# The second FFN of a transformer layer: eight blocks of ten, not five, by seven products for eight

## The chip, the cores and the metric

The kernel runs on one core of a Trainium2 chip. The metric is the device time of one execution in microseconds (us). TensorE (PE) multiplies matrices, VectorE (DVE) and ScalarE (ACT) work on tiles element by element, GpSimd (POOL) and SyncE (SP) here mostly issue transfers (DMA). SBUF is the memory on the chip, PSUM the small memory in banks into which TensorE sums.

## The reference

One layer of a diffusion backbone, width 2048, with 256 context tokens and 256 latent tokens: a half step of a gated FFN, a token mixer (attention heads and mLSTM heads), another half step FFN, and an RMSNorm. Each part is modulated by shift, scale and gate vectors (`mod`, nine of them) made from a condition vector. The change is about the second FFN, which is computed for the 256 latent tokens alone:

```python
def adaln(x, g, mod, i):
    return rms_norm(x, g) * (1 + mod[:, i + 1, None, :]) + mod[:, i, None, :]

def half_step_ffn(x, mod, i, g, w_up, w_down):
    h = adaln(x, g, mod, i)
    a, b = jnp.split(h @ w_up, 2, axis=-1)
    return x + 0.5 * mod[:, i + 2, None, :] * ((jax.nn.silu(a) * b) @ w_down)
```

`w_up` is 2048 x 11264 and `w_down` 5632 x 2048, in fp32. `mod` vector 8 is the gate of the second FFN.

## The kernel before

**Numbers.** An fp32 operand is kept as the sum of two parts: `hi`, a rounded copy, and `lo`, the rest. A product of two operands takes three matmuls (`mm3`, L145 to L149: hi by hi, hi by lo, lo by hi). Weights arrive by DMA in pieces of 128x2048 (1024 KB, tile `raw`, three buffers); `split` (L117) makes from each half a `hi` by ScalarE (L125) and a `lo` by VectorE (L126). There are four buffers of each, so two whole pieces. `load_split` (L138) does the load and the split, and steps one item of whatever stands in `beside["load"]`.

**Order.** The program is written out by hand with generators: a main loop goes through units of TensorE's work, and side generators are stepped at each of them (`steps`, `drain`, `weave`). A scheduler then puts each engine's instructions in an order that is fixed before the run.

**Modulation vectors.** A `mod` vector is a product of the condition with its own weights; it is computed by VectorE in 32 items of 128x1024 (`mod_half`, L200; the operation is on L205, with a read of its accumulator). Vectors 5 to 7 are computed beside the mixer by the class `Beside` (L271): 96 items, each with a DMA of 512 KB into one of a few slots (`fetch`, L287), paced by the table `PACE` of (item, step) pairs over 188 steps. The items and their loads are pinned in the order of the program. Vector 8 is computed in the second FFN, by `mod_late` (L264): 32 items in `beside["load"]`.

**The mixer** (about 1346 to 1945 us) projects, runs convolutions, the mLSTM and the attention, and ends in an output projection. Small operations of it that the change touches: the scaling of the mLSTM's values (`vw`, L1429), the copy of its state (L1434), the scaling of its queries (`mqT`, L1552), the scaling of attention's probabilities (L1699), and a copy of the heads' output (`cx`, L1750), all by VectorE.

**The second FFN** (L1935 to L2310) has 5632 hidden channels in eleven blocks of 512. Block 0 starts while the mixer ends; block 10 is finished last, with the final norm. Each block needs an up projection (two matrices a and b, 2048 x 512 each) and a down projection (512 x 2048, four pieces).
- `up(n)`: eight units, each one weight piece and 24 matmuls of 128x512; the two halves of the 256 tokens go to two banks. 192 matmuls.
- `quad(n)`: the same by seven products for eight, after Strassen and Winograd, on quarters of the tokens and channels: the weights come as sums of quarters. The seven products are a11, a12, n1, s4, s2, s3, a22, in this order, each in two steps of 12 matmuls (one weight piece of 128x2048 for each), so 14 steps and 168 matmuls. They sum in two banks X and Y (`psx`, one buffer each): a11 in X; a12 in Y; n1 in Y, s4 added in Y; s2 and s3 added in X; a22 in Y. After each product the bank is read: X copied by ScalarE (p1), Y added to it by VectorE (c11), Y copied by ScalarE (`cy`, L2098, kept), copied again (p35), X added by VectorE (c12), X added by VectorE and copied by ScalarE (c22), Y added by VectorE (c21), with silu and products in between (L2084, L2085, L2094, L2117).
- The weight sums of a quad are made by DMA: two tiles `chain` are loaded by SP, and GpSimd issues loads that add to them (`accum`, L735): three sums for the chain and one for the tile `ra`, for each of two pieces, so eight a quad. The first load of the next quad's chain is issued at the end (`again`).
- `turned` (L2051 on) transposes a block's result by TensorE and splits it into `hid2h` (ScalarE, L2066) and `hid2l` (VectorE, L2068, L2070); these tiles have two buffers.
- `down(n)`: four units of 24 matmuls; each pair of banks is added to `acc2` by VectorE (L2208), eight adds of 128x512 a block (block 0 is copied by ScalarE).

PSUM has four banks `mm`, two `tr` for the transposes, X and Y. The quads are the odd blocks 1 to 9, the `up` blocks 2, 4, 6, 8, 10. The main loop goes through 73 units of up and down, and `PACE2 = 70 / 73` puts one of the 70 quad steps behind each unit.

Of the kernel before, what the change touches and what calls it, by code (L numbers as in the profile page):

```python
# [19 lines left out]
P = 128  # L20
D = 2048
# [14 lines left out]
PACE = (4, 2), (12, 13), (19, 19), (26, 28), (33, 37), (37, 44), (42, 51), (48, 54), (52, 61), (55, 70), (58, 76), (59, 85), (63, 96)  # L36
PACE += (70, 102), (72, 109), (75, 118), (76, 130), (77, 144), (80, 152), (83, 163), (85, 166), (86, 174), (96, 181)

PACE2 = 70 / 73
# [17 lines left out]
def tile_layer(ctx: ExitStack, tc: tile.TileContext, I: dict, out: bass.AP):  # L57
# [205 lines left out]

    def mod_late(sp, i0, i1, pace):  # L264

        cB = sp.tile([P, 1024], F32, name="cBl", bufs=1)
        cond = Conditions(lambda h: h, lambda h: conditions({LAT: cB}, h, h + 1, (LAT,)), lambda h: {LAT: cB})
        raws = lambda: sp.tile([P, 1024], F32, tag="sraw", name="sraw", bufs=2)
        return mod_items(half_items(i0, i1), nc.sync.dma_start, raws, 2, cond, None, pace)
# [989 lines left out]
    with ExitStack() as mx:  # L1259
# [31 lines left out]
        N_EARLY, N_MIXER = 50, 85  # L1291

        early2 = one([P, 2, 1024], "early2", tag="mqT")
        tiles = [(mm.tile([P, 1024], F32, name="sr0"), 96)] + [(mm2.tile([P, 1024], F32, name=f"sr{j}"), N_MIXER) for j in (1, 2)]
        tiles += [(x, N_EARLY) for x in (early2[:, 0, :], early2[:, 1, :], one([P, 1024], "early1", tag="rt"))]
        mods = Beside(mm, 5, 8, tiles, PACE)
# [122 lines left out]
        def state(h, kTc):  # L1419
# [7 lines left out]
            for t in range(2):  # L1427
                for d in range(2):
                    nc.vector.tensor_scalar(vw[:, t, d, :], v1[CTX][t][:, h, :], wg[:, t, d, h : h + 1], None, op0=ALU.mult)  # L1429
# [4 lines left out]
            nc.vector.tensor_copy(C1[:, h, :, :], b[:, :260].rearrange("p (d c) -> p d c", d=2))  # L1434
# [39 lines left out]
        def latents():  # L1474
            held = {}
            for h in range(NH + 1):
                if h < NH:
# [31 lines left out]
                    nc.vector.tensor_tensor(A, A, mqT[:, h, :].unsqueeze(1).to_broadcast([P, 2, T]), op=ALU.mult)  # L1509
                    for d in range(2):  # L1510

                        for w, p0 in ((slice(0, 2), 0), (slice(2, 3), 3)) if d == 0 else ((slice(0, 1), 0), (slice(1, 3), 2)):
                            e_ = E[:, d, w, :]
                            nc.vector.tensor_tensor(e_, e_, pS.rearrange("p (q c) -> p q c", q=4)[:, p0 : p0 + w.stop - w.start, :], op=ALU.mult)
# [26 lines left out]
        for h in range(NH):  # L1541
# [8 lines left out]
            nc.scalar.activation(y, y, AF.Silu)  # L1550

            nc.vector.tensor_scalar(mqT[:, h, :], y, ISQ, None, op0=ALU.mult)  # L1552
# [130 lines left out]
        def attention(kv):  # L1683
            items = [(t, g) for t in range(2) for g in range(4)]
            pr, pT, o = {}, {}, {}
            for i in range(len(items) + 2):
                if i < len(items):
# [11 lines left out]
                    nc.vector.tensor_scalar(p, p, sd, None, op0=ALU.mult)  # L1699
# [42 lines left out]
        def mlstm_cat(c):  # L1742

            for t in range(2):
# [5 lines left out]
                nc.vector.tensor_copy(cxs[c, t], tb)  # L1750
# [36 lines left out]
        mods.more([(late2[:, 0, :], 96), (late2[:, 1, :], 96), (one([P, 1024], "late1", tag="C1"), 96)], nc.sync)  # L1787
# [147 lines left out]
    with f2x:  # L1935
        def hid_tiles():

            return [f2.tile([P, FB, T], F32R, tag=g, name=g) for g in ("hid2h", "hid2l")]
# [47 lines left out]
        acc2 = f2.tile([P, 2, D], F32, name="acc2", bufs=1)  # L1986
        chain_ = [f3.tile([P, 2048], F32, tag=f"c{q}", name=f"chain2{q}") for q in range(2)]
        f8cm = pool(name="f8", bufs=1)
        beside["load"] = mod_late(f8cm.__enter__(), 8, 9, ((32, 62),))
# [3 lines left out]
        QUADS = range(1, LAST, 2)  # L1993
# [57 lines left out]
        def turned():  # L2051
# [4 lines left out]
            if n >= 2 and n - 2 not in summed or n - 1 not in hids or (n - 1, 0) in [x[:2] for x in turn] or (n - 1, 1) in [x[:2] for x in turn]:  # L2056
                return
            turn.pop(0)
            if n not in hids:
                hids[n] = hid_tiles()  # L2060
# [18 lines left out]
        def ca_tile():  # L2079
            return f2b.tile([P, CB], F32, tag="ca", name="ca")  # L2080

        def quad(n):
# [26 lines left out]
            def c22():  # L2109
                assert (n, 0) in done  # L2110
# [13 lines left out]
            def again(q):  # L2124
                if n + 2 in QUADS:
                    nc.sync.dma_start(chain_[q], part(n + 2, 0, q))

            def loaded(q):
                ra[q] = ra_tile()
# [278 lines left out]
```

## Time and profile before

| what | us |
| --- | --- |
| median of 3 runs (least to most) | 2613.49 (2612.78 to 2615.28) |
| the profiled execution, its span from first to last instruction | 2612.7 |
| TensorE busy in it | 2590.1 |
| VectorE busy | 2119.7 |
| ScalarE busy | 1364.8 |
| mixer, output projection and start of the second FFN | about 1346 to 1945 |
| main part of the second FFN and final norm | about 1945 to 2613 |

The profiled execution has no time of its own beside its span. Its granted clock is 0.996 of full speed. The profile has a page (busy time by engine, the chain of work that ended last, groups of instructions by line) and a trace that can be asked for waits, stretches of time and timelines. In a row of a group stand the line, the engine, the operation with output and inputs and their sizes, the count, then the busy time in us and the mean of one in ns, then the engine's idle time ahead of them and what ended it. In a row of a line stand the least, median and longest duration in ns. In a row of waits stand the total in us, the number and the longest. Matmuls overlap in the pipeline, so their distance from start to start counts, not their length.

### The profile page before, as it was taken

The numbers are of one execution on the slowest core, as the hardware profiler recorded it, in microseconds if no ns is written. First come the engines' busy times: TensorE is split into PE (matmuls) and PEld (weight loads), VectorE is DVE, ScalarE is ACT, GpSimd is POOL, SyncE is SP. The second block draws the span as 40 slices with busy tenths as digits, with TensorE's granted clock in tenths as the row PEclk, the third lists the DMA queues.
The fourth block names the chain that finished last, engine by engine and source line by source line (L and its number), as shares of the span: only waits on it lengthen the run. The fifth ranks groups of instructions, "written<-read, shape, count | busy, mean of one in ns | idle before, by whom it ended". The sixth has DMA issues, their size and how long they took to land.

```text
span 2612.7 us, 33775 instructions
## 1 busy us (share of the span) xinstructions
PE 2590.1 (99%) x12742; PEld 2158.4 (83%) x12742; DVE 2119.7 (81%) x2860; ACT 1364.8 (52%) x1734; POOL 205.2 (8%) x261
## 2 busy tenths in 40 slices
PE   8999999999999999999999999999999999999998
PEld 5788888888888888888889889888898888888887
DVE  7788888878888788888887879788888777777867
ACT  4454444454444465444454337555576655555554
POOL 0000000100000100010110000120000000000001
PEclk8999999999999999999999999999999999999999
DMA  9989999999999998889987856665679998989975
GB/s 389 353 215 266 280 273 274 257 273 284 265 277 277 271 246 237 231 200 232 231 247 262 300 193 236 220 214 208 236 254 302 309 293 278 286 285 283 270 231 174
DMA packets 127219, 679.97 MB, mean 260 GB/s; under 512 B 14152, under 2 KB 16712, under 8 KB 65232
## 3 DMA queue, kind: packets, MB, share of 16 engines
q1 hardware_dynamic: 99696, 500.59, 51.6%
q0 software_dynamic: 27360, 177.22, 34.7%
q8 instruction: 100, 1.64, 0.2%
q14 instruction: 63, 0.52, 0.1%
HBM read 659.87 MB, written 17.89 MB: 259 GB/s over the span
## 4 chain that ended last, share of the span: by engine, by line
PE 92%; DVE 3%; DMA 2%; issue 1%; ACT 1%; POOL 0%; ACTq 0%; POOLq 0%; SPq 0%; DVEq 0%
PE mm L147 24%; PE mm L149 24%; PE mm L148 24%; PE mm L85 2%; PE tr L147 2%; PE tr L149 2%; PE tr L148 2%; PE Y L149 1%; PE Y L147 1%; PE Y L148 1%; PE tr L85 1%; PE X L147 1%; PE X L149 1%; PE X L148 1%; DVE lo L126 1%
## 5 line engine op out<-in xcount | busy, mean ns | idle before, releaser
L125 ACT ACTIVATE hi<-raw 128x1024 fp32r<-128x1024 f32 (+3 forms) x536 | 556.4, 1042 | 594.7 <-PE mm L149 435.4
L126 DVE TENSOR_TENSOR lo<-raw,hi 128x1024 fp32r<-128x1024 f32 (+1 forms) x524 | 632.1, 1211 | 272.3 <-ACT hi L125 246.9
L125 ACT ACTIVATE hi<-chain 128x1024 fp32r<-128x1024 f32 x320 | 338.0, 1059 | 257.3 <-PE mm L149 133.9
L126 DVE TENSOR_TENSOR lo<-chain,hi 128x1024 fp32r<-128x1024 f32 x320 | 386.5, 1221 | 85.4 <-ACT hi L125 82.3
L147 PE MATMUL mm<-hi,hhi 128*128 128x512 f32 (+3 forms) x1024 | 393.8, 385 | 0.0
L148 PE MATMUL mm<-lo,hhi 128*128 128x512 f32 (+3 forms) x1024 | 386.8, 378 | 0.0
L149 PE MATMUL mm<-hi,hlo 128*128 128x512 f32 (+3 forms) x1024 | 386.8, 378 | 0.0
L205 DVE SCALAR_TENSOR_TENSOR junk<-sraw,cBh 128x1024 fp8e5<-128x1024 f32 x192 | 234.4, 1221 | 16.8 <-DMA sraw<-in_w_mt 14.4
L149 PEld LDWEIGHTS mm<-hi,hlo 128*128 128x128 f32 x1024 | 192.5, 188 | 33.9
L147 PEld LDWEIGHTS mm<-hi,hhi 128*128 128x128 f32 x1024 | 192.6, 188 | 31.0
L148 PEld LDWEIGHTS mm<-lo,hhi 128*128 128x128 f32 x1024 | 192.8, 188 | 30.6
L149 PE MATMUL mm<-hi,hid2l 128*128 128x512 f32 x352 | 137.4, 390 | 0.0
L147 PE MATMUL mm<-hi,hid2h 128*128 128x512 f32 x352 | 137.2, 390 | 0.0
L148 PE MATMUL mm<-lo,hid2h 128*128 128x512 f32 x352 | 137.1, 389 | 0.0
L148 PE MATMUL mm<-lo,h2hi 128*128 128x512 f32 x320 | 124.9, 390 | 0.6 <-DVE lo L126 0.6
L147 PE MATMUL mm<-hi,h2hi 128*128 128x512 f32 x320 | 124.8, 390 | 0.0
L149 PE MATMUL mm<-hi,h2lo 128*128 128x512 f32 x320 | 124.6, 389 | 0.0
L735 POOL DMA_DIRECT2D chain<-in_w_up1b x60 | 53.1, 886 | 726.4 <-DVE lo L126 699.5
L147 PE MATMUL mm<-hhi,hi 128*128 128x512 f32 (+1 forms) x288 | 101.1, 351 | 0.0
L149 PE MATMUL mm<-hhi,lo 128*128 128x512 f32 (+1 forms) x288 | 99.0, 344 | 0.0
L148 PE MATMUL mm<-hlo,hi 128*128 128x512 f32 (+1 forms) x288 | 98.8, 343 | 0.0
L205 DVE SCALAR_TENSOR_TENSOR sr<-sr,cBl 128x1024 f32<-128x1024 f32 x65 | 78.4, 1219 | 9.0 <-DMA sr<-in_w_mt 9.0
(517 smaller groups left out, 5466.9 us busy)
## 6 DMA issues: line engine op xcount, KB each, us to landing
raw<-in_w_dn SPq DMA_DIRECT2D x70, 1024.0 KB, 7.7
sraw<-in_w_mt SPq DMA_DIRECT2D x128, 512.0 KB, 7.7
chain<-in_w_up1b POOLq DMA_DIRECT2D x60, 1024.0 KB, 10.4
raw<-in_w_up2b SPq DMA_DIRECT2D x50, 1024.0 KB, 6.9
raw<-in_w_up1b SPq DMA_DIRECT2D x40, 1024.0 KB, 7.7
mraw<-in_w_m SPq DMA_DIRECT2D x32, 1024.0 KB, 7.8
sr<-in_w_mt SPq DMA_DIRECT2D x62, 512.0 KB, 5.4
chain<-in_w_dn POOLq DMA_DIRECT2D x30, 1024.0 KB, 9.4
```

What stands on the lines that cost most here:

```text
L85: ins = getattr(self.engine, name)(*a, **k)
L125: scalar[0].activation(hi, src, AF.Copy)
L126: vector[0].tensor_tensor(lo, src, hi.bitcast(F32), op=ALU.subtract)
L147: tensor[0].matmul(out_ap, sh, mh, start=first, stop=False, skip_group_check=skip)
L148: tensor[0].matmul(out_ap, sh, ml, start=False, stop=False, skip_group_check=skip)
L149: tensor[0].matmul(out_ap, sl, mh, start=False, stop=last, skip_group_check=skip)
L205: ins = nc.vector.scalar_tensor_tensor(junk() if junk else raw, raw, 1.0, cB[s], op0=ALU.mult, op1=ALU.mult, accum_out=mT[:, i, s, kt, h : ...
L735: accum = lambda dst, src: nc.gpsimd.dma_start(dst, src, accum_op=ALU.add)
```

## The change

- The quads are blocks 1, 2, 4, 5, 6, 7, 8, 9; `up` is left for blocks 3 and 10. The main loop has 48 units: up(3), down of 0 and 1, of 2 and 3, of 4 and 5, up(10), down of 6 and 7. After two units, 112 quad steps are spread over the other 46. The last down, of 8 and 9, follows.
- `down` takes two blocks and sums both in one pair of banks, so that `acc2` is added to half as often.
- One of a quad's weight sums is made by VectorE (`ahead` loads `ra` early, `summed_half` adds it to the chain in halves of 128x1024, at the steps listed in `between`). A quad has six adding DMAs for eight.
- `hid2h` and `hid2l` have three buffers, `ca` three.
- Vector 8 is computed in the mixer: `Beside` has 128 items for 96, with a new `PACE`; `mod_late` goes.
- In the mixer `vw`, the state copy, the probabilities' scale and `cx` go to ScalarE; the queries' scale is put into two operations of VectorE that follow anyway.

```diff
+N_HID = 3
...
+PACE = (4, 2), (12, 13), (19, 19), (27, 28), (35, 37), (41, 44), (49, 51), (56, 54), (62, 61), (67, 70), (70, 76), (71, 85), (76, 96)
+PACE += (83, 102), (87, 109), (91, 118), (94, 130), (97, 144), (101, 152), (107, 163), (110, 170), (128, 181)
...
-PACE2 = 70 / 73
...
-        N_EARLY, N_MIXER = 50, 85
+        N_EARLY, N_MIXER = 62, 109
...
-        mods = Beside(mm, 5, 8, tiles, PACE)
+        mods = Beside(mm, 5, 9, tiles, PACE)
...
-                    nc.vector.tensor_scalar(vw[:, t, d, :], v1[CTX][t][:, h, :], wg[:, t, d, h : h + 1], None, op0=ALU.mult)
+                    nc.scalar.activation(vw[:, t, d, :], v1[CTX][t][:, h, :], AF.Copy, scale=wg[:, t, d, h : h + 1])
...
-            nc.vector.tensor_copy(C1[:, h, :, :], b[:, :260].rearrange("p (d c) -> p d c", d=2))
+            nc.scalar.activation(C1[:, h, :, :], b[:, :260].rearrange("p (d c) -> p d c", d=2), AF.Copy)
...
-                    nc.vector.tensor_tensor(A, A, mqT[:, h, :].unsqueeze(1).to_broadcast([P, 2, T]), op=ALU.mult)
+                    nc.vector.scalar_tensor_tensor(A, A, ISQ, mqT[:, h, :].unsqueeze(1).to_broadcast([P, 2, T]), op0=ALU.mult, op1=ALU.mult)
...
-            nc.vector.tensor_scalar(mqT[:, h, :], y, ISQ, None, op0=ALU.mult)
+            nc.scalar.activation(mqT[:, h, :], y, AF.Silu)
...
-                    nc.vector.tensor_scalar(p, p, sd, None, op0=ALU.mult)
+                    nc.scalar.activation(p, p, AF.Copy, scale=sd)
...
-                nc.vector.tensor_copy(cxs[c, t], tb)
+                nc.scalar.activation(cxs[c, t], tb, AF.Copy)
...
-        beside["load"] = mod_late(f8cm.__enter__(), 8, 9, ((32, 62),))
...
-        QUADS = range(1, LAST, 2)
+        QUADS = tuple(n for n in range(1, LAST) if n != 3)
...
+            def ahead(q):
+                ra[q] = ra_tile()
+                nc.sync.dma_start(ra[q], part(n, 1, 2 + q))
+
+            def summed_half(q, h):
+                w = slice(h * 1024, (h + 1) * 1024)
+                add(chain_[q][:, w], chain_[q][:, w], ra[q][:, w])
+                if h:
+                    accum(ra[q], part(n, 1, q))
+
+            between = {(2, 1): (0, 0), (3, 0): (0, 1), (3, 1): (1, 0), (4, 0): (1, 1)}
...
-                (a12, plain, "Y", True, None, c11),
-                (n1, held, "Y", True, chained(1, 2), kept),
-                (s4, loaded, "Y", False, lambda q: accum(ra[q], part(n, 1, q)), p35),
+                (a12, plain, "Y", True, ahead, c11),
+                (n1, held, "Y", True, None, kept),
+                (s4, lambda q: ra[q], "Y", False, None, p35),
...
         def units():
-            yield from up(2)
-            yield from down(0)
-            for n in (4, 6, 8):
-                yield from up(n)
-                yield from down(n - 3)
-                yield from down(n - 2)
-            yield from down(7)
-            yield from up(10)
-            yield from down(8)
+            yield from up(3)
+            for n in (0, 2, 4):
+                yield from down(n, n + 1)
+            yield from up(LAST)
+            yield from down(6, 7)
+
+        N_UNITS, N_FIRST = 2 * 8 + 4 * 8, 2
...
-            while n_side < n_quads and n_side < (u + 1) * PACE2:
+            while n_side < n_quads * (u + 1 - N_FIRST) / (N_UNITS - N_FIRST):
                 next(side)
                 n_side += 1
                 turned()
...
-        drain(down(LAST - 1))
+        drain(down(LAST - 2, LAST - 1))
```

More of the change, by code (lines that the diff above doesn't have):

```diff
@@ L2055, in turned @@
             n, t, sa, sign = turn[0]
[L2056 to L2057 removed]
+            if n not in hids:
+                if n - 1 not in hids or len(hids) - len(summed) >= N_HID:
+                    return
+                hids[n] = hid_tiles()
             turn.pop(0)
[L2059 to L2060 removed]
             tb = tbank()
@@ L2183, in up, with block @@
                     yield
-        def block(n, wt, t):
-            b = bank()
+        def block(b, n, wt, t, first=True, last=True):
             tt = slice(t * P, (t + 1) * P)
@@ L2190, in block, with down @@
                 w = slice(j * CB, (j + 1) * CB)
[L2191 removed]
+                mm3(b, hids[n][0][:, j, tt], hids[n][1][:, j, tt], *wt(w), first and j == 0, last and j == FB - 1)
             return b
         late = {}
[L2196 to L2198 removed]
+        def down(*ns):
             for cb in range(NCB):
[L2200 to L2214 removed]
```

76 lines of the change are left out of this document (32 added, 44 removed).

## Prediction

> **What bounds the kernel now.** I read the page first: busy time by engine, and the chain of work that ended last by engine.
>
> ```profile
> span 2612.7 us, 33775 instructions
> PE 2590.1 (99%) x12742; PEld 2158.4 (83%) x12742; DVE 2119.7 (81%) x2860; ACT 1364.8 (52%) x1734; POOL 205.2 (8%) x261
> ...
> PE 92%; DVE 3%; DMA 2%; issue 1%; ACT 1%; POOL 0%; ACTq 0%; POOLq 0%; SPq 0%; DVEq 0%
> ```
>
> TensorE (PE) is busy for 99% of the span, and 92% of the chain is its work. So a change is worth what it takes from TensorE's queue, less the waits that it puts there. The second view is the list of TensorE's waits, for the second FFN (1945 us to the end) alone:
>
> ```profile
> PE mm L148 <- DVE lo L126: 0.6, 1, 0.6
> ```
>
> That is its only row. For the mixer and what stands about it (1346 to 1945 us) the same list has two:
>
> ```profile
> PE mm L449 <- ACT hi L125: 0.4, 1, 0.4
> PE tr L380 <- DVE acc L1193: 0.3, 1, 0.3
> ```
>
> The third view, busy time by stretch, says how near the other engines are (PE, PEld, DVE, ACT, POOL, granted clock, DMA share, GB/s):
>
> ```profile
> 1945.00:1980.00 35.00, 34.39 (x152) 27.95 (x151) 34.92 (x34) 23.41 (x26) 1.84 (x2) 1.00 0.87 275
> 1980.00:2050.00 70.00, 70.00 (x315) 57.71 (x314) 52.21 (x53) 42.74 (x49) 5.22 (x6) 1.00 1.01 316
> 2050.00:2150.00 100.00, 100.00 (x446) 82.64 (x445) 75.29 (x81) 55.80 (x58) 6.98 (x8) 1.00 0.96 282
> 2150.00:2250.00 100.00, 100.00 (x449) 82.63 (x448) 73.27 (x75) 56.90 (x60) 5.21 (x6) 1.00 0.89 282
> 2250.00:2350.00 100.00, 100.00 (x450) 82.72 (x449) 78.32 (x86) 55.80 (x58) 5.21 (x6) 1.00 0.90 290
> 2350.00:2450.00 100.00, 100.00 (x450) 82.69 (x449) 80.33 (x89) 54.56 (x57) 5.27 (x7) 1.00 0.93 279
> 2450.00:2510.00 60.00, 60.00 (x268) 49.58 (x267) 44.48 (x49) 34.42 (x36) 5.23 (x6) 1.00 0.97 266
> ```
>
> TensorE is full at a granted clock of 1.00. VectorE (DVE) stands at 73 to 80%, ScalarE (ACT) at 56%, the DMA engines at about 0.93. VectorE and the DMA are close behind; whether they stay behind is the question.
>
> **The change part by part.**
>
> *Matmuls.* A block by seven products has 7 x 24 = 168 matmuls of 128x512, a block by eight has 192. Before: 5 x 168 + 5 x 192 = 1800. After: 8 x 168 + 2 x 192 = 1728. So 72 go; the down projections keep theirs, summed in a bank or not, and so do the transposes. The spacing comes from the timeline, of which these are the first and the last row of 8 matmuls in a row:
>
> ```profile
> 2470.41 0.39 PE L149 MATMUL Y<-hi,n1f 128*128 128x512 f32 x1
> ...
> 2472.00 0.39 PE L147 MATMUL mm<-hi,h2hi 128*128 128x512 f32 x1
> ```
>
> (2472.00 - 2470.41) / 7 = 0.227 us. All 72 lie in a full TensorE queue, so the gain is 72 x 0.227 = **16.3 us**. [...]
>
> *The bank turnovers (the term against).* Each quad sums in two banks, X and Y, of one buffer each. Between two of its products ScalarE or VectorE must read the bank before TensorE writes on. Before, there was a unit of an up or down block (24 matmuls, 5.4 us) between any two steps, which hid every read. Now 112 quad steps go over 46 units, 2.4 per unit, so steps follow each other directly. What a read takes is seen behind the n1 matmul of 2470.41 above:
>
> ```profile
> 2470.84 0.60 ACT L2098 ACTIVATE cy<-Y 128x512 f32<-128x512 f32 x1 [0.30 <-PE Y L149]
> ...
> L2084 DVE TENSOR_TENSOR ca<-Y,ca 128x512 f32<-128x512 f32 x10 | 6.8, 684 | 0.0
> ```
>
> The next slot of TensorE was 2470.64; the read ended at 2471.44, and a semaphore must still pass (0.05 us, my estimate): 0.85 us lost if nothing stands between. For VectorE's read of 0.68 us the same comes to 0.93 us, plus what it is still busy with: half of a 1.2 us operation, most of the time, about 0.4 us on the mean, so 1.3 us. I counted the matmuls between in the new order of TensorE's queue:
> - n1 to s4 (ScalarE reads Y): none in quads 1 and 6, two (0.46 us) in quads 4, 5, 8, 9, a unit in 2 and 7: 2 x 0.85 + 4 x 0.4 = 3.3 us.
> - a12 to n1 (VectorE reads Y): two in quads 1, 5, 6, 9, a unit or more elsewhere: 4 x (1.3 - 0.46) = 3.4 us.
> - s2 to s3 (VectorE reads X): five (1.13 us) in quads 2, 4, 7, 8, else a unit: 4 x 0.2 = 0.8 us.
> - a22 to the transposes of its result (an add, a silu, a product, about 2.6 us by such rows): 2.7 us at the least: nothing.
>
> Sum **7.5 us**. The lower end is 4 us (a read by VectorE that starts at once); the upper end is 14 near places, each behind one more 1.2 us operation: 7.5 + 17 = 24 us. [...] No row of before shows such a wait, since the cover was there.
>
> *VectorE in the second FFN.* The rows:
>
> ```profile
> L126 DVE TENSOR_TENSOR lo<-raw,hi 128x1024 fp32r<-128x1024 f32 x182 | 221.8, 1224 | 127.6 <-ACT hi L125 126.9
> ...
> L2208 DVE TENSOR_TENSOR acc<-acc,mm 128x512 f32<-128x512 f32 x72 | 49.1, 681 | 1.9 <-PE mm L149 1.8
> ...
> L125 ACT ACTIVATE hi<-raw 128x1024 fp32r<-128x1024 f32 x182 | 192.0, 1060 | 208.9 <-PE mm L149 178.7 <-DMA raw<-in_w_up2b 10.8 <-DMA raw<-in_w_dn 6.7
> ...
> L205 DVE SCALAR_TENSOR_TENSOR sraw<-sraw,cBl 128x1024 f32<-128x1024 f32 x32 | 39.0, 1219 | 0.0
> ```
>
> A quad splits 14 weight pieces (28 lo operations), an up block 8 (16): 220 before, 256 after, so 36 x 1.22 = +44 us. The four half sums of ra into the chain per quad, 32 of 128x1024, at the price of lo: +39. The reads and products, 6 per quad and 2 per up: 40 before, 52 after: +8. The paired down blocks: 40 fewer acc adds: -27. The gate's items gone to the mixer: 32 x (1.22 + 0.08 for reading the accumulator): -42. Net **+22 us**. VectorE's 404 us in the 530 us from 1980 to 2510 (76%) become about 426 in 521 (82%). While quads run it is denser: a quad's share of the queue is 14 steps and 46 / 8 = 5.75 units, 306 matmuls or 69.5 us and the transposes, about 70.5; VectorE's is 39.5 lo and 4 sums of 1.22 us and some 13 operations of 0.68, 62 us, 88%. The idle column says how it is hidden: VectorE sat 127 us waiting for ScalarE's hi, mostly and ScalarE mostly for TensorE to free a buffer (its row is the third), so these splits run ahead. I cost it at **0**; the 12% that are left are the cover, and what goes beyond them shows. ScalarE gains 36 hi of 1.06 and 12 of 0.6, +45 us on 56%: nothing.
>
> *DMA.* In the window from 1945 us, by queue, by issue, and the issue itself on GpSimd (ns, least, median, most):
>
> ```profile
> q1 hardware_dynamic: 21737, 135.49, 53.3%
> q0 software_dynamic: 6912, 44.04, 34.3%
> ...
> chain<-in_w_up2b POOLq DMA_DIRECT2D x30, 1024.0 KB, 11.0
> ...
> chain<-in_w_up2b SPq DMA_DIRECT2D x8, 1024.0 KB, 6.2
> ...
> L735 POOL DMA_DIRECT2D chain<-in_w_up2b x30: 861/876/961, 1951.8 to 2498.8; - x30
> ```
>
> Of 668 us that is 2.63 us per MB by the hardware queue and 5.20 by the accumulating one; a 1024 KB piece (1.05 MB) takes 2.8 or 5.5 us. Weights by hardware go from 114 pieces to 108, the gate's 16 pieces' worth goes, accumulates go from 40 to 48 (six per quad, not eight): -22 x 2.8 + 8 x 5.5 = -18 us. The share stays near 0.93; without VectorE's sum it would have been 16 x 5.5 = 88 us more. What is tight is latency: an accumulate has 16.8 us from the step that reads the old chain to the one that reads the new (a11 to n1 in quad 2; before at least 32), and 11.0 of landing, 0.9 of issue and the split of 2.3 need 14.2. The chain's reload between quads lands in 6.2 us, and three times has 5.4 to 8.2 us (24 to 36 matmuls). I take **1 us**, from 0 to 8 x 3 = 24 us if each quad's chain comes 3 us late.
>
> *The gate in the mixer.* 32 items of 1.30 us join VectorE's mixer, while small operations go to ScalarE:
>
> ```profile
> L205 DVE SCALAR_TENSOR_TENSOR sr<-sr,cBl 128x1024 f32<-128x1024 f32 x65 | 78.4, 1219 | 9.0 <-DMA sr<-in_w_mt 9.0
> ...
> L1429 DVE TENSOR_SCALAR vw<-v1c,wg x32: 275/281/286, 1469.1 to 1560.6; 128x130 f32<-128x130 f32 x32
> ...
> L1434 DVE COPY C<-mm x8: 420/422/422, 1492.8 to 1576.3; 128x260 f32<-128x260 f32 x8
> ...
> L1552 DVE TENSOR_SCALAR mqT<-cy x8: 285/292/295, 1579.6 to 1629.1; 128x256 f32<-128x256 f32 x8
> ...
> L1699 DVE TENSOR_SCALAR pr<-pr,sd x16: 477/486/489, 1737.0 to 1827.9; 128x512 f32<-128x512 f32 x16
> ...
> 1580.00:1640.00 60.00, 60.00 (x422) 56.43 (x422) 54.50 (x130) 42.09 (x74) 2.76 (x6) 1.00 0.68 232
> ...
> 1800.00:1840.00 40.00, 39.98 (x226) 33.87 (x225) 30.85 (x58) 22.33 (x37) 0.00 (x0) 1.00 0.49 170
> 1840.00:1870.00 30.00, 30.00 (x134) 24.86 (x133) 25.15 (x36) 11.84 (x13) 0.00 (x0) 1.00 0.75 259
> ```
>
> +41.6 us, less 32 x 0.28, 8 x 0.42, 8 x 0.29, 16 x 0.49 and four copies of cx at the 0.68 of any 512 wide read: +16 us net in some 520 us. The items are pinned: one whose weights are late holds all of VectorE's queue behind it, the splits too. The first row shows that this occurs (9.0 us over four items) and that TensorE, two splits ahead, did not feel it. The new pace puts 18 items where 10.5 were, in the last eleven steps of the out projection. 1800 to 1870 us is 56 of 70 us now; 7.5 x 1.3 - 2 for the moved scales makes it 64, 91%, and the last 30 us touch 100% (five more items: 25.15 + 6.5). I take **1 us**, from 0 to 25, which is the 41.6 that nothing pays for (41.6 - 16 moved by ScalarE).
>
> *Sum* against the profiled execution's span: 2612.7 - 16.3 + 7.5 + 1 + 1 = 2605.9 us. The median of the runs, 2613.5, stands 0.8 above that span, so the forecast for it is **2606.7 us**.
>
> **The rivals.**
>
> *A. The turnovers are nearly free.* Pro: VectorE's reads in the row of L2084 had no idle time ahead of them, but it was idle 130 us elsewhere, so it may be there at once; ScalarE was, with 0.30 us idle. Con: ScalarE's 0.85 us needs no busy engine. Then 2613.5 - 16.3 + 4 = **2601 us** or a little less.
>
> *B. The quads starve.* At 88% VectorE, and the accumulates with 16.8 us where 14.2 are needed, each of eight quads loses 1.4 us or more besides: 2606.7 + 8 x 1.4 = **2618 us**, no gain. Pro: share 0.93 of the DMA, the single chain pieces. Con: from 1945 to 1980 VectorE was 34.92 of 35 us busy and TensorE lost 0.6 us.
>
> *C. The mixer pays (slower).* The pinned gate items with late weights hold the splits; TensorE waits once VectorE is behind by more than two splits (some 5 us). It decides from there: at 91 to 100% that backlog does not melt. Of the 41.6 us up to 25 surface: 2606.7 + 25 = **2632 us**. Con: 1580 to 1640 us, which before the change has VectorE at 54.5 of 60, shows no wait.
>
> *D. The change does not do what it says:* it would, if the matmuls were not fewer; they are, by 72 in the order of the queue. Time 2613; nearly excluded.
>
> **How the numbers follow.** Forecast (2602 to 2611) 0.42, A 0.23, B 0.21, C 0.12, D 0.02. Some 0.2%, 5 us, is what a measurement of this kernel can tell from no change: faster means under 2608.3, slower over 2618.7. Faster: all of A and nine tenths of the forecast, 0.62 with rounding; same: the rest of the forecast, D, and most of B, 0.23; slower: C and the end of B, 0.15. The range takes in A down to 2598 (all terms of loss at 1 us) and B up to 2618, and leaves out C.
>
> **What would show it.** In the new trace TensorE's matmuls in the second FFN are 72 fewer at the same 0.227 us. Its list of waits, so far one row there, shows "Y" behind ScalarE's cy copy and VectorE's ca add, some 0.4 to 0.9 us each, 7 to 8 us in all; if those rows hold under 4, A is right. Waits for lo from the chain, or hi for a DMA of chain, mean B. Rows between 1800 and 1870 us, or any in the mixer, over 5 us mean C. I am wrong if TensorE's pitch changes, or if the waits lie in none of these places.

## The result, and the profile after

The changed kernel takes 2631.5 us (median of 4 runs, 2627.3 to 2632.8) where the kernel before takes 2613.5: 1.0068 of the time, 95% interval 1.0055 to 1.0081. It is slower by 18 us; 2606.7 was forecast, and the range ended at 2618.

The page of the changed kernel, the same lines as those shown of before:

```profile
span 2630.2 us, 33776 instructions
PE 2584.3 (98%) x12670; PEld 2142.3 (81%) x12670; DVE 2159.7 (82%) x2832; ACT 1433.9 (55%) x1846; POOL 216.2 (8%) x269
...
PE 81%; DMA 7%; DVE 6%; issue 3%; ACT 2%; POOL 0%; SPq 0%; ACTq 0%; POOLq 0%; DVEq 0%
```

TensorE has 72 instructions less (12742 to 12670), as counted, and the span is 17.5 us longer. Busy shares say nothing of it. The chain does: TensorE's part fell from 92 to 81%, and DMA and VectorE have 13% between them, 5% before. TensorE's waits in the second FFN, from 1945 us to the end (line waited for: us in total, times, longest), have six rows where there was one:

```profile
PE tr L2052 <- DVE ca L2074: 6.5, 6, 1.8
PE mm L148 <- DVE lo L126: 3.8, 6, 0.8
PE mm L147 <- ACT hi L125: 2.5, 4, 0.8
PE Y L147 <- DVE ca L2073: 2.2, 3, 0.9
PE Y L147 <- ACT cy L2087: 2.1, 6, 0.7
PE X L148 <- DVE lo L126: 1.9, 3, 0.7
```

(Line 2052 of the changed kernel is the transposes' line 2063 of before, 2087 is 2098, 2073 and 2074 are 2084 and 2085.) The list counts a wait only from the modelled end of the matmul before it. The loss is read from the starts in the timeline: all that the distance of two matmuls has above 0.227 us. Summed where it is over 0.1 us, that is 1.3 us in the second FFN before, and 28.3 us after: 7.5 at the transposes, 3.3 at s4, 3.4 at n1, 8.1 behind lo, 3.2 behind hi, and 2.8 of small ones behind these. These sums are called pauses below; by unrounded starts they come out up to 1 us smaller.

Two more marks divide the span: the first matmul of the mixer (`mm<-hi,hhi`) and the first with the second FFN's input (`mm<-hi,h2hi`). They and the last matmul of the span, after:

```profile
1366.21 0.37 PE L147 MATMUL mm<-hi,hhi 128*128 128x256 f32 x1
...
1950.14 0.40 PE L147 MATMUL mm<-hi,h2hi 128*128 128x512 f32 x1
...
2619.75 0.39 PE L149 MATMUL mm<-hi,hid2l 128*128 128x512 f32 x1
```

Before:

```profile
1367.58 0.36 PE L147 MATMUL mm<-hi,hhi 128*128 128x256 f32 x1
...
1944.70 0.40 PE L147 MATMUL mm<-hi,h2hi 128*128 128x512 f32 x1
...
2603.01 0.39 PE L149 MATMUL mm<-hi,hid2l 128*128 128x512 f32 x1
```

So the mixer's stretch grew from 577.1 to 583.9 us (+6.8), and the second FFN's from 658.3 to 669.6 (+11.3: 16.3 of matmuls gone, 27.0 of pauses come, 0.6 of smaller ones). The rest, -1.4 ahead of the mixer and +0.7 behind the last matmul, lies outside both.

Where the pauses in the second FFN come from is read one queue further back. ScalarE's waits there after the change have a row that before does not have at all:

```profile
ACT hi L125 <- PE mm L149: 111.0, 86, 3.0
ACT hi L125 <- DMA chain<-in_w_up2b: 26.8, 13, 3.9
```

Each of the waits over 1 us among these 13 stands where one quad ends and the next begins. Ten of the 13, with 23 of the 27 us, are for the reload, the load of the next quad's chain; the other three, 3.5 us, are for adding DMAs. The reload is issued when a22 has read the old chain, and lands 6.8 us later (median of the 13 whose landing the trace has; 5.5 to 9.7). One such end, quad 4, on ScalarE, on VectorE and on TensorE:

```profile
2182.90 2.01 ACT L125 ACTIVATE hi<-chain 128x1024 fp32r<-128x1024 f32 x2 [2.69 <-DMA chain<-in_w_up2b]
2184.81 0.61 ACT L2105 ACTIVATE ca<-ca 128x512 f32<-128x512 f32 x1
```

```profile
2181.80 0.69 DVE L2073 TENSOR_TENSOR ca<-Y,ca 128x512 f32<-128x512 f32 x1 [0.33 <-PE Y L149]
2183.99 1.23 DVE L126 TENSOR_TENSOR lo<-chain,hi 128x1024 fp32r<-128x1024 f32 x1 [1.50 <-ACT hi L125]
2185.46 0.69 DVE L2074 TENSOR_TENSOR ca<-ca,cy 128x512 f32<-128x512 f32 x1 [0.24 <-ACT ca L2105]
```

```profile
2184.09 0.39 PE L149 MATMUL mm<-hi,hid2l 128*128 128x512 f32 x1
2186.30 0.41 PE L2052 MATMUL tr<-ident,ca 128*128 128x128 f32 x2 [1.82 <-DVE ca L2074]
```

VectorE's sum was done at 2182.5. The silu that follows it on ScalarE could have begun then. But ahead of it in ScalarE's queue stood the next quad's hi<-chain, waiting for its weights; the silu began at 2184.8, the product at 2185.5, and the transposes 2.0 us late. A late load has here held up work that does not need it. The DMA engines were not full: their share from 1980 to 2510 us is 0.85, where near 0.93 was forecast.

### The profile page after: what moved, and what is told of

Read it like the earlier page. It is cut to its first block, busy times and chain, and to the rows that moved or that the text cites. A ratio compares the mean times of both kernels' runs of the same rounds, so it can differ in the third digit from the quotient of the medians.

```text
span 2630.2 us, 33776 instructions
## 1 busy us (share of the span) xinstructions
PE 2584.3 (98%) x12670; PEld 2142.3 (81%) x12670; DVE 2159.7 (82%) x2832; ACT 1433.9 (55%) x1846; POOL 216.2 (8%) x269
## 4 chain that ended last, share of the span: by engine, by line
PE 81%; DMA 7%; DVE 6%; issue 3%; ACT 2%; POOL 0%; SPq 0%; ACTq 0%; POOLq 0%; DVEq 0%
PE mm L148 21%; PE mm L149 21%; PE mm L147 20%; DVE lo L126 3%; PE mm L85 2%; DMA chain<-in_w_up2b 2%; PE Y L147 2%; PE Y L148 1%; PE Y L149 1%; ACT hi L125 1%; DMA mraw<-in_w_m 1%; PE tr L148 1%; PE tr L149 1%; PE tr L147 1%; PE X L149 1%
## 5 line engine op out<-in xcount | busy, mean ns | idle before, releaser
L125 ACT ACTIVATE hi<-raw 128x1024 fp32r<-128x1024 f32 (+2 forms) x500 | 517.2, 1040 | 441.8 <-PE mm L149 278.4
L126 DVE TENSOR_TENSOR lo<-raw,hi 128x1024 fp32r<-128x1024 f32 (+2 forms) x488 | 584.4, 1207 | 176.5 <-ACT hi L125 153.7
L125 ACT ACTIVATE hi<-chain 128x1024 fp32r<-128x1024 f32 x368 | 388.1, 1059 | 325.8 <-PE mm L149 185.4
L126 DVE TENSOR_TENSOR lo<-chain,hi 128x1024 fp32r<-128x1024 f32 x368 | 445.4, 1221 | 139.8 <-ACT hi L125 136.1
L205 DVE SCALAR_TENSOR_TENSOR junk<-sraw,cBh 128x1024 fp8e5<-128x1024 f32 x192 | 234.3, 1221 | 22.8 <-DMA sraw<-in_w_mt 20.5
L205 DVE SCALAR_TENSOR_TENSOR sr<-sr,cBl 128x1024 f32<-128x1024 f32 x85 | 102.5, 1216 | 14.9 <-DMA sr<-in_w_mt 14.8
L125 ACT ACTIVATE hi<-ra 128x1024 fp32r<-128x1024 f32 x64 | 67.9, 1061 | 53.6 <-PE mm L149 31.7
L126 DVE TENSOR_TENSOR lo<-ra,hi 128x1024 fp32r<-128x1024 f32 x64 | 77.5, 1222 | 21.1 <-ACT hi L125 19.6
L148 PEld LDWEIGHTS mm<-lo,hid2h 128*128 128x128 f32 x352 | 66.1, 188 | 18.5 <-DVE lo L126 5.1
```

Of the source, the lines that this page charges most:

```text
L125: scalar[0].activation(hi, src, AF.Copy)
L126: vector[0].tensor_tensor(lo, src, hi.bitcast(F32), op=ALU.subtract)
L148: tensor[0].matmul(out_ap, sh, ml, start=False, stop=False, skip_group_check=skip)
L205: ins = nc.vector.scalar_tensor_tensor(junk() if junk else raw, raw, 1.0, cB[s], op0=ALU.mult, op1=ALU.mult, accum_out=mT[:, i, s, kt, h : ...
```

## The experiments

Fifteen kernels ran, each beside new runs of the kernel before (medians 2613.1, 2613.9, 2614.1 and 2613.9 us). Theory Q: the second FFN's new pauses are the reload and the bank turnovers, so a matter of where the quad steps stand. Rival V: VectorE has too much to do. Rival M: the mixer pays most of it. The last four columns are from the one execution of each kernel that was profiled: its span, the mixer's stretch and the second FFN's as above, and its pauses. That execution need not be a typical one. The span is some 1.7 us less than the time of the same execution, so t_pace and t_pace_forms were profiled in the fastest of their runs (t_pace's ten go from 2608.9 to 2621.9 us), t_gate in the slowest, and t_swap 2.5 us above its median.

| kernel | median us | ratio (95%) | span | mixer | second FFN | pauses |
| --- | --- | --- | --- | --- | --- | --- |
| before | 2613.5 | | 2612.7 | 577.1 | 658.3 | 1.3 |
| after | 2631.5 | 1.0068 (1.0055 to 1.0081) | 2630.2 | 583.9 | 669.6 | 28.3 |
| t_mixer | 2618.3 | 1.0018 (1.0009 to 1.0028) | 2616.5 | 582.8 | 657.4 | 0.7 |
| t_moved | 2616.8 | 1.0013 (1.0004 to 1.0022) | 2615.3 | 579.1 | 658.1 | 1.2 |
| t_gate | 2619.7 | 1.0024 (1.0014 to 1.0034) | 2621.4 | 587.6 | 657.2 | 0.4 |
| t_pscale | 2632.6 | 1.0074 (1.0059 to 1.0089) | 2627.5 | 581.7 | 669.1 | 27.5 |
| t_nogate | 2628.1 | 1.0057 (1.0042 to 1.0072) | 2628.4 | 580.5 | 670.8 | 29.4 |
| t_nogate_pscale | 2628.8 | 1.0055 (1.0039 to 1.0071) | 2628.0 | 579.5 | 672.9 | 31.7 |
| t_swap | 2621.8 | 1.0033 (1.0022 to 1.0044) | 2622.6 | 581.7 | 665.1 | 24.0 |
| t_nosum | 2640.8 | 1.0110 (1.0095 to 1.0125) | 2639.3 | 582.4 | 680.8 | 39.1 |
| t_pace | 2612.8 | 0.9999 (0.9990 to 1.0009) | 2607.2 | 581.9 | 651.1 | 10.0 |
| t_swappace | 2611.5 | 0.9991 (0.9982 to 1.0000) | 2608.0 | 581.1 | 647.9 | 6.9 |
| t_pace_forms | 2615.0 | 1.0000 (0.9991 to 1.0009) | 2606.8 | 581.2 | 650.4 | 9.2 |
| t_exchange_pace | 2616.6 | 1.0010 (1.0001 to 1.0020) | 2617.4 | 581.6 | 658.6 | 17.2 |
| t_best | 2614.4 | 1.0007 (0.9997 to 1.0016) | 2614.3 | 582.5 | 656.3 | 15.0 |
| t_seven_swap | 2626.8 | 1.0055 (1.0038 to 1.0072) | 2624.4 | 580.6 | 666.4 | 19.7 |
| t_seven_pace | 2624.0 | 1.0035 (1.0022 to 1.0047) | 2620.8 | 584.2 | 661.5 | 15.2 |

The mixer's stretch of the ten kernels with the same mixer (after, t_mixer, t_swap, t_nosum, t_pace, t_swappace, t_pace_forms, t_exchange_pace, t_seven_swap, t_seven_pace) lies between 580.6 and 584.2, so a difference under 4 us in one profile says little. The three longest, after, t_mixer and t_seven_pace, are those in which the granted clock was 0.50 for 3.4 us in the attention (see the last section).

**The mixer's part alone**, on the kernel before (all of the diff's mixer lines, and in the second FFN):

```diff
-        beside["load"] = mod_late(f8cm.__enter__(), 8, 9, ((32, 62),))
```

> The kernel before with only the mixer's part of the change: the gate's 32 items beside the mixer with the new pace, the small operations moved to ScalarE; the second FFN as before, without its gate items. The traces of before and after, laid side by side, put the start of the second FFN 5.4 us later after the change (matmul mm<-hi,h2hi at 1944.70 and 1950.14 us). If that is the mixer's own loss, this kernel takes 2613.5 + 5.4 = 2619 us, and the second FFN's length stays. Rival (the mixer's loss is paid back because VectorE is freed of 32 items in the second FFN, or the loss belongs to the later FFN's first loads): 2613 to 2615 us.

It takes 2618.3 us, 5.2 us more than the runs of before beside it (4.7 by the ratio), and the second FFN without its gate items is no shorter to speak of (657.4). The mixer's loss is real and is its own: rival M holds for about 5 of the 18 us, not for most.

**The exchange of buffers**, chain and ra (in `quad`, and `chain_` with four tiles, of which two were ra's):

```diff
+            own = 2 * (QUADS.index(n) % 2)
+            held_ = chain_[own : own + 2]
+            other = chain_[2 - own : 4 - own]
...
-                ra[q] = ra_tile()
+                ra[q] = other[q]
...
-                (s3, lambda q: ra[q], "X", False, None, c22),
-                (a22, held, "Y", True, again, c21),
+                (s3, lambda q: ra[q], "X", False, again, c22),
+                (a22, held, "Y", True, None, c21),
```

> The changed kernel with chain and ra exchanging their buffers from quad to quad: the next quad's first weight piece is loaded into ra's buffer, free from s3 on, rather than into the chain's, free only when a22 has been split. Nothing else changes, no operation is added. Theory Q (the reload): of the second FFN's 28 us of TensorE's pauses some 7.5 at the transposes of a22's result and most of 7.6 + 3.2 behind lo and hi come from ScalarE's hi<-chain, which waits for the reload (27 us in 13 waits) with c21's silu behind it; these go, 11 to 16 us: 2616 to 2620 us. The turnovers n1 to s4 and a12 to n1, 7 us, stay. Rival V (VectorE, 88% busy while quads run, is behind whatever the load does): under 4 us gained, 2628 us or more.

2621.8 us, 10 us back; 11 to 16 were expected. TensorE's waits in its second FFN:

```profile
PE mm L147 <- ACT hi L125: 4.8, 3, 2.5
PE mm L148 <- DVE lo L126: 4.1, 7, 0.8
PE Y L147 <- ACT cy L2093: 2.1, 6, 0.7
PE Y L147 <- DVE ca L2076: 1.9, 3, 0.9
```

The row of the transposes, 6.5 us, is gone altogether, and of ScalarE's 13 waits for chain two remain (1.85 and 0.75 us). That the late reload held c21's work is shown. The turnovers stayed as they were (2.1 and 1.9). But the waits for hi grew from 2.5 to 4.8, now for raw pieces that land late, and in the profiled execution the pauses fell by 4.3 us only. Two things stand behind that: this execution was 2.5 us above the median, and some 4.4 us of its 24.0 are matmuls that started 0.43 us apart at a granted clock of 0.50 (from 2124.7 to 2128.2 us and from 2418.3 to 2425.1), which the second FFN of the changed kernel's profile does not have.

**The sum given back to the DMA** (`accum(1,2)` on the chain, `ra` loaded at s4, no `summed_half`):

```diff
-                (a12, plain, "Y", True, ahead, c11),
-                (n1, held, "Y", True, None, kept),
-                (s4, lambda q: ra[q], "Y", False, None, p35),
+                (a12, plain, "Y", True, None, c11),
+                (n1, held, "Y", True, chained(1, 2), kept),
+                (s4, loaded, "Y", False, lambda q: accum(ra[q], part(n, 1, q)), p35),
```

> The changed kernel with the weight sum of VectorE given back to the adding DMA (eight a quad again): 32 half sums of 1.22 us leave VectorE, 16 adding pieces of 5.5 us join the DMA. Theory Q and a DMA that is nearly full: later chains and reloads, slower by 5 to 40 us, 2637 to 2670 us. Rival V: VectorE is what is behind, so faster by 5 to 10 us, 2622 to 2626 us.

9 us slower than the change, with VectorE freed of 39 us of work. ScalarE's waits for chain grew from 26.8 to 46.7 us. The run alone doesn't part the two, as it loads the DMA while it frees VectorE; but with t_pace below, which leaves VectorE's work as it is and gains 18.7 us, rival V in its plain form, VectorE's sum of work as the bound, falls.

**The units at the turnovers.** The rule that spreads the steps evenly is replaced by a list; a unit stands behind a12, n1, s2 and s3, two behind a22:

```diff
+        GROUPS = [4, 2, 4, 2, 2, 0] * 7 + [4, 2, 4, 4]
...
-            while n_side < n_quads * (u + 1 - N_FIRST) / (N_UNITS - N_FIRST):
+            while n_side < sum(GROUPS[: max(0, u + 1 - N_FIRST)]):
```

> The changed kernel with the 112 quad steps spread over the same 46 units another way: a unit always stands behind a12, n1, s2, s3 and a22 (two behind a22), and steps follow each other directly only where the bank changes or nothing reads it. Theory B (the turnovers n1 to s4 and a12 to n1, 3.3 + 3.4 us in the trace, are bank waits and nothing else): they go, and with two units behind a22 the reload has 10.9 us, so part of the 19 us that hang on it goes too; 2616 to 2624 us. Rival R: what the fixed pattern gives at the turnovers it takes from the adding DMAs, whose time from one chain's reading to the next falls to 13.6 us where 14.2 are needed; 2628 us or more, with waits for chain behind n1 and a22 in ScalarE's list.

2612.8 us: 18.7 us back by two lines that move no work from one engine to another. TensorE's waits in the second FFN, and ScalarE's for weights:

```profile
PE X L147 <- ACT s3f L2006: 3.7, 1, 3.7
PE Y L148 <- DVE lo L126: 1.4, 2, 0.8
PE tr L2052 <- DVE ca L2074: 0.8, 1, 0.8
PE X L149 <- DVE s3f L2001: 0.5, 1, 0.5
```

```profile
ACT hi L125 <- DMA chain<-in_w_up2b: 9.2, 4, 3.9
ACT hi L125 <- DMA raw<-in_w_dn: 5.8, 2, 3.2
```

Both rows of Y, the turnovers, are gone, and ScalarE's waits for chain fell from 26.8 to 9.2 us. None of these is for the reload any more: between the end of a22's step on a piece and the start of a11's step of the next quad there are now 14.1 us, where 2.7 to 11.2 were. All four are for adding DMAs, and those grew from 3.5 to 9.2 us. So what rival R feared, the adding DMAs late instead, did come, but it cost TensorE next to nothing in seven of eight quads and some 3 us in the last, and R's price, 2628 us or more, falls. The largest wait left is a new one, for the last token form, which the new order asks for earlier. In this profile, the fastest of ten runs, the second FFN is 7.2 us shorter than before the change and the mixer 4.8 longer; by the medians the whole gains nothing over the kernel before.

**Both together**, with the token forms one per unit as they were (t_swappace) and two per unit (t_exchange_pace); the units at the turnovers with two forms per unit, without the exchange (t_pace_forms); and all of it with a changed mixer (t_best: the probabilities' scale and cx back on VectorE, and fewer gate items in the attention):

```diff
-            steps(forms)
+            steps(forms, 2)
...
-PACE += (83, 102), (87, 109), (91, 118), (94, 130), (97, 144), (101, 152), (107, 163), (110, 170), (128, 181)
+PACE += (83, 102), (87, 109), (91, 118), (96, 130), (101, 144), (102, 152), (104, 163), (110, 170), (128, 181)
```

> Both: chain and ra exchange buffers, and the units stand at the turnovers. If the two causes add up (10 us by the exchange, 7 us by the turnovers), 2613 to 2616 us. If the adding DMAs are late by the fixed pattern, 2620 us or more.

> Exchange of buffers and units at the turnovers, as before, but with the token forms made in the first two units, so that the exchanged buffers do not overwrite the last of them. The second FFN from its first matmul to its last is 658.3 us before, 669.6 after, 651.1 with the units at the turnovers, 647.9 with both; 640.7 would be the 72 matmuls fewer and no pause. Expected: 646 to 650 us, 2610 to 2612 us in all. If the earlier forms collide with the first quad: over 652 us.

> The changed kernel with the units at the turnovers, and the token forms made in the first two units, no exchange of buffers. In the version with the forms one per unit TensorE waited 3.9 us for the last form (s3f), of 10 us of pauses in the second FFN. Expected: 651.1 - 4 = 647 us for the second FFN, 2609 us in all. If making them early holds VectorE's splits: 2612 us or more.

> The same, with the mixer eased: the probabilities' scale and the copies of cx back on VectorE, and the gate's items paced so that only 3 stand in the attention's steps 144 to 163 (10 in the changed kernel). If the mixer's loss of 5 us is the meeting of items and softmax, 2 to 4 us come back: 2606 to 2609 us, faster than the kernel before. If it is VectorE's sum of work, nothing comes back: 2611 to 2614 us.

t_swappace (in it, and in t_seven_swap below, the exchanged buffer overwrites the last token form, so s3's sums are others) takes 2611.5 us, t_exchange_pace 2616.6, t_pace_forms 2615.0, t_best 2614.4. The two causes don't add up to 17 us: what the list does includes most of what the exchange does. The earlier forms took s3f's wait away (no row of it in t_pace_forms) and put as much elsewhere: the waits for lo grew from 1.4 to 5.4 us, the longest 1.5. In t_exchange_pace ScalarE waits 15.6 us for chain and 9.8 for `ra`. The two tiles change places there, and all nine of these waits are for adding DMAs: 25.4 us, where t_pace has 9.2 and t_swap 2.6. The longest adding DMA took 20.6 us to land, 18.2 in t_pace. That the reload, which the exchange sends out while they run, slows them would fit, and wasn't tried. Three of these four expectations were too low by some 5 to 7 us, and the slower case that each of them named is the nearer one. None beats the kernel before beyond doubt.

**Seven quads**, evenly spaced and with the exchange (t_seven_swap), or with one unit behind every product (t_seven_pace, whose list is shown); up(7) comes behind down(2, 3):

```diff
-        QUADS = tuple(n for n in range(1, LAST) if n != 3)
+        QUADS = tuple(n for n in range(1, LAST) if n not in (3, 7))
...
+        GROUPS = [2, 2, 2, 2, 2, 2, 2, 0] * 6 + [2, 2, 2, 2, 2, 2, 2]
```

> The changed kernel with the exchange of buffers and seven quads for eight (block 7 by eight products again): 24 matmuls more, 5.4 us, but 98 steps over 56 units, 1.75 per unit rather than 2.4. If the second FFN's remaining 24 us of pauses come from the density of the steps (banks, VectorE, adding DMAs), they fall by more than half, 2612 to 2616 us. If they come from raw loads that are late in any case, 2622 to 2626 us.

> Seven quads for eight (block 7 by eight products), the changed buffers, and one unit behind every product, so 8 units a quad. 24 matmuls more than eight quads, 5.4 us; every reload, adding DMA and bank read has a unit as cover, as before the change. If the pauses are a matter of where the steps stand, the second FFN takes 640.7 + 5.4 = 646 us and up to 3 of pauses, 2607 to 2611 us in all, faster than the kernel before; if they come from the total of DMA or VectorE work, 655 us and more, 2616 us or more.

2626.8 and 2624.0 us: both miss what was hoped for, and come out near the other case of their expectations. Chain and turnovers are nearly quiet, but ScalarE waits for raw pieces; for t_seven_pace:

```profile
ACT hi L125 <- DMA raw<-in_w_dn: 11.5, 4, 4.3
...
ACT hi L125 <- DMA raw<-in_w_up2b: 6.9, 3, 3.1
```

The kernel before has as much of such waits up to 2585 us, 10.8 and 6.7, and loses next to nothing by them; here three of them (at 1975, 2151 and 2320 us) are followed by pauses of TensorE of 1.0 to 2.2 us. With 3.7 us for the last token form again, and some 3 us of matmuls at a granted clock of 0.50, its pauses are 15 us. So the order of the steps isn't all. That these loads are issued late behind others that wait in SP's queue would fit, and wasn't tried.

**Parting the mixer's loss**, from after (the scale back on VectorE; the gate's items left out; both) and from before (the moved operations alone; the gate's items alone):

```diff
-                    nc.scalar.activation(p, p, AF.Copy, scale=sd)
+                    nc.vector.tensor_scalar(p, p, sd, None, op0=ALU.mult)
...
-        mods = Beside(mm, 5, 9, tiles, PACE)
+        mods = Beside(mm, 5, 8, tiles, PACE)
```

> The changed kernel with the scale of attention's probabilities (16 operations of 128x512) back on VectorE. Theory S: in the mixer the scale stands in ScalarE's queue behind a split's hi and between two exponentials, so TensorE's transposes of p wait (1.05 and 2.15 us in the trace) and run slowly behind the pause; with it undone some 4 us come back, 2627 us, and the two rows of waits go. Rival L: the waits come from gate items whose weights land late and hold VectorE (0.5 us of such idle time stands right ahead); then the waits stay, and the time is 2631 us or more, as VectorE gets 16 x 0.49 us more work.

> The changed kernel with the gate's 32 items left out altogether (its place is taken by another modulation vector, so the output isn't the reference's) and the mixer's items paced as before; the small operations stay on ScalarE. It parts the mixer's loss of some 5 us. Theory G: it is the items, which stand in VectorE's queue between the reduction, the reciprocal and the splits of the attention's first blocks; then TensorE's waits at the transposes of p go, the second FFN starts at 1945 us rather than 1950, and the time is 2626 to 2627 us. Rival S: it is the operations moved to ScalarE; then the waits stay and the time is 2631 us.

> The changed kernel without the gate's items (another modulation vector in its place, so the output isn't the reference's) and with the scale of attention's probabilities back on VectorE. From the mixer's first matmul to the second FFN's first one it is 577.1 us before, 583.9 after (581 to 584 in six kernels with the same mixer), 580.5 without the gate's items, 581.7 with the scale undone. If the two block each other (the items fill VectorE, the scale fills ScalarE, each alone leaves the softmax late), both undone give 577 to 578.5 us. If a third of the moved operations is the cause (the copies of cx, of the state, the values' scale), the stretch stays at 580 us.

> The kernel before with only the mixer's small operations moved to ScalarE or folded; the gate stays in the second FFN. It parts the mixer's 5 us from the other side. If the moved operations are the cause (without the gate's items 580.5 us of the mixer's stretch were left, 3.4 above before): 2616 to 2617 us. If they are harmless without the items: 2613 to 2614 us.

> The kernel before with only the gate's 32 items moved beside the mixer (new pace, more slots' turns); all small operations stay on VectorE. If items and softmax meet on VectorE: 2617 to 2622 us, as nothing is taken from VectorE for them. If the moved operations alone cost: 2613 to 2615 us.

On the kernel before, the gate's items alone cost 5.8 us by the medians, the moved operations alone 2.9, both together 5.2. They do not add up, though with intervals of some 2.5 us to each side that is near the edge of the noise: it looks as if moving the operations gives back a part of what the items cost, and costs something itself. From the other side, leaving the items out of the changed kernel gives 3.4 us (the intervals overlap), and the scale alone nothing: TensorE's waits at the transposes of p are 3.9 us in t_pscale, so theory S falls and rival L stands. In the profile of the changed kernel TensorE's waits in the mixer rose from 0.7 to 5.2 us, and 1.7 more are matmuls at half the granted clock behind the longest of them; that is nearly all of the 6.8. The largest place is the attention's start, where the changed kernel has

```profile
PE tr L1696 <- ACT pr L1690: 3.0, 2, 2.1
```

and, in VectorE's queue at that place, two items of modulation vectors (L205) between a reduction and the reciprocal of the same softmax, the second of them late by its load. Before the change one item stands there. (The items at this place belong to vector 7; the gate's 32 make the whole row of items denser.)

```profile
1742.62 0.68 DVE L1684 TENSOR_REDUCE nm<-mm 128x1 f32<-128x512 f32 x1
1743.22 1.22 DVE L205 SCALAR_TENSOR_TENSOR sr<-sr,cBl 128x1024 f32<-128x1024 f32 x1
1744.36 0.08 DVE L205 DVE_READ_ACCUMULATOR sr<-sr,cBl 128x1 f32 x1
1744.36 0.15 DVE L1685 TENSOR_SCALAR nm<-nm 128x1 f32<-128x1 f32 x1
1745.03 1.23 DVE L205 SCALAR_TENSOR_TENSOR sr<-sr,cBl 128x1024 f32<-128x1024 f32 x1 [0.52 <-DMA sr<-in_w_mt]
...
1747.32 0.15 DVE L1689 RECIPROCAL sd<-sd 128x1 f32<-128x1 f32 x1
```

ScalarE's scaling of p waits for that reciprocal, and the transposes for the scaling:

```profile
1747.51 0.72 ACT L1690 ACTIVATE pr<-pr,sd 128x512 f32<-128x512 f32 x1 [2.12 <-DVE sd L1689]
```

Without the items (t_nogate) both waits at this place go, and one of 1.9 us comes at 1767 us, where t_moved, with the operations moved and no items, has one of 1.2. With items and scale both undone the waits there go (t_nogate_pscale has 0.6 us), and about half of the stretch's loss with them (579.5 us, where kernels with the same mixer have 580.6 to 584.2 and before has 577.1). But t_best, which moved items out of the attention, got no shorter (582.5): its waits at the transposes fell to 1.5 us, and others grew. So the loss is shown to be the mixer's, and the medians point to the items first; that their place in the attention is the cause is not shown.

## Why the prediction was wrong

By its own steps:
- *Matmuls, -16.3.* Right: 72 fewer at 0.227 us; t_pace_forms' 650.4 us less its 9.2 of pauses is 641, that is 658.3 - 1.3 - 16.3.
- *Turnovers, 7.5.* Right: 3.3 at s4 as forecast (0.85 twice, 0.40 four times), 3.4 at n1 as forecast and in the four quads named; nothing at s3 for 0.8. The list of t_pace took them away. n1 and s4 write to the very sums that are read; in the changed kernel's trace they start 0.053 to 0.056 us after the end of the read, at all ten places, where 0.05 had been estimated.
- *a22 to the transposes, nothing.* Wrong: 7.5 us. The work takes not 2.6 us but 3.5 where nothing is in its way (from the end of a22's last slot to the end of the product, in seven of t_pace's eight quads; 3.3 to 3.7 before the change), so that the shortest cover, 2.7 us, was too short by itself. The larger part is what stood ahead of its silu in ScalarE's queue, the wait for the reload, which wasn't counted: with it the work took up to 7.0 us. This is the step that failed in kind: a wait was added, and I did not name what is queued behind it.
- *DMA, 1 us.* Wrong, and it is the same cause: I had written that the reload has 5.4 to 8.2 us three times where it needs 6.2 of landing, and still costed it at 1. Its landing was 6.8, and ScalarE waited 23 us for it. That the 7.5 us at the transposes hang on it is shown by t_swap, in which they went with it. The 11 us behind lo and hi did not go there; t_pace took most of them away, and how much of them is the reload, how much other late loads and splits that follow each other closely, stays open. Rival B had the place; its price, 1.4 us a quad, was too small.
- *VectorE, 0.* Right as a sum (t_pace, with the same work on VectorE), not quite in place: where several steps of 12 matmuls (2.72 us) follow each other, each needs two lo from VectorE, 1.13 us apart, and a sum or a read besides. From 2083 to 2090 us in the changed kernel VectorE goes from one to the next with 0.1 us of rest in all, and TensorE pauses 0.7 us for it.
- *Mixer, 1.* Wrong by size: 5 us (6.8 in the profile). I looked for it in the out projection, where VectorE would be fullest. TensorE has no wait there (1800 to 1870 us); 4.7 of the 6.8 us fell in the attention (3.0 of waits and 1.7 at the lower clock), where small steps that TensorE waits for follow each other. Fullness was the wrong measure; which measure is right t_best leaves open.

So rivals B and C both came true in part, and my chances gave 0.15 to slower. That C's time, 2632 us, is nearly the measured one is chance: C put 25 us in the mixer, where 5 were.

## What to carry to other kernels

When work is packed closer, count for each pair of neighbours what used to stand between them, and price the wait with all that is queued behind it on each engine in order, not with the one operation that needs the data. Where steps can be put in a list, put the filler where a bank is read or a buffer is reloaded: here that was worth 18.7 us with the same work, while even spacing lost more than 72 matmuls brought. And an operation that is off the path by its sum of time can still stand in a short chain of dependent steps: look for it there, though here moving it away (t_best) won nothing.

## What the runs showed of the hardware

A pause of 2 us cost twice here. Behind the 2.07 us wait at 1748 us in the attention, TensorE's matmuls start 0.43 us apart rather than 0.23, for some 3 us, and the granted clock, 0.50 from 1749.50 to 1752.91 us, is low there (PE, PEld, DVE, ACT, POOL, clock, DMA, GB/s):

```profile
1748.00:1750.00 2.00, 1.72 (x12) 1.63 (x13) 2.00 (x4) 1.66 (x3) 0.00 (x0) 0.87 0.84 317
1750.00:1752.00 2.00, 2.00 (x7) 1.52 (x6) 0.66 (x3) 1.24 (x3) 0.00 (x0) 0.50 0.92 311
1752.00:1754.00 2.00, 2.00 (x8) 1.61 (x7) 0.00 (x0) 0.27 (x2) 0.00 (x0) 0.77 1.04 399
```

That is about 1.7 us more. In t_swap a wait of 2.5 us was followed by a clock of 0.50 as well, from 2418 to 2425 us; the 1.82 us wait at 2186 us in the changed kernel was not, nor were waits of 2.03 us (t_pace) and 2.70 us (t_nosum) at the same place in the attention.

So in these runs the length of one wait didn't decide it. In every trace with more than one, the changes of the clock between the mixer's start and the end of the second FFN stand a multiple of 3.41 us apart, and each low stretch lasts 3.41 or 6.83 us. Cut into such steps and summed over the seventeen profiled executions, every step with more than 1.9 us without TensorE at work (by the profile's modelled ends), of those that ran at 1.00, is followed by a step at 0.50 (14 of 14), none with less than 1.6 is, and between these 5 of 13 are. In the changed kernel the step from 1746.1 us has 2.07 us without TensorE at work and 0.50 behind it, the one from 2183.0 us has 1.82 us and 1.00 behind it.
